# A shorter TensorE program in the experts' stage: one form of transposes, 512-wide gate and up products, one copy of the last down

## The chip, the core and the metric

The kernel runs on one core of one Trainium2 chip. The metric is the device time of one execution in microseconds; the time before is the median of three runs. The five engines each run a program of their own and meet at semaphores: TensorE (PE; its weight loads are shown apart as PEld), VectorE (DVE), ScalarE (ACT), GpSimd (POOL) and SyncE (SP). Line numbers are those of the kernel before.

## The reference

One layer of an encoder on 1024 tokens of width 1024 in float32: a mixer (neighbourhood attention, a bidirectional RWKV-7 scan, pooling), two layer norms, and a mixture of experts. Only the last is touched. Each token goes to two of 32 experts; the tokens of an expert are padded to blocks.

```python
order = jnp.argsort(e_flat)                      # assignments sorted by expert
padded = ((counts + MOE_BLOCK - 1) // MOE_BLOCK) * MOE_BLOCK
...
def expert_block(args):
    ti, e, wt = args
    xb = x_pad[ti]                               # the block's token rows, width 1024
    hb = jax.nn.silu(xb @ w_gate[e]) * (xb @ w_up[e])      # 1024 -> 512
    return (hb @ w_down[e]) * wt[:, None]                  # 512 -> 1024
y = lax.map(expert_block, (...))
out = jax.ops.segment_sum(y.reshape(total, d), buf_tok, num_segments=t + 1)[:t]
```

## The kernel before

The mixer and the router fill the first 949 us of the profiled span and are left as they are. Then `experts()` (line 1461) runs up to NP = 50 blocks. How many are used, and how many token rows each holds, is known only at run time: the router writes a code for each block (0 unused, 1 for 32 rows, 2 for 64, 3 for 128), and `size(e, g)` (line 1498) reads it into a register on every engine. The program is written out block after block, for each engine by itself; nothing loops. Wherever the work depends on the block's size, `by_size` (line 1511) writes it three times, for 128, 64 and 32 rows in this order, each behind a compare-and-branch that skips it when the code differs. The first SURE = 16 blocks are always used; from block 15 on, `go_on` (line 1516) tests whether the next block is used: its false side holds `end()`, which on PE is one more copy of the last block's down products in all three sizes, and its true side the next step, nested inside.

`pipeline` (line 1528) sets PE's order in step g:

1. `size(g+1)` (line 1499);
2. `head(g)`: gate and up products. For 128 rows (line 1689) two halves of 256 columns, each gate then up, 8 matmuls each into one PSUM bank; for 64 and 32 rows (line 1697) the token columns share the array, 16 and 32 matmuls;
3. `rows(g+1)` (line 1672): eight transposes of the gathered token rows, as many rows wide as the block;
4. `down(g-1)` (line 1717 for 128 rows, line 1728 for the others): 8, 8 or 16 matmuls;
5. `turn(g)` (line 1705): transposes of h = silu(gate)*up, four, four or two, in a shape of its own for 128 rows and for the smaller sizes.

A float32 matmul is two matmul records with a weight load each in the trace; a transpose is one of each. On ACT, `head` is the silu (lines 1765, 1768) and `turn` the copy of h's transpose out of PSUM (line 1773); on DVE, `head` is the product (lines 1789, 1793), and `out` scales the block's result into y (lines 1751, 1756). Both copy half of the token transposes (line 1738). Their semaphores count two updates for each block on `sil` and `h`.

SP loads the weights of block g into buffer set g % 3, gate, up (line 1559) and then the down matrix of block g-1, each 2 MB, with at most two under way (line 1558); a load whose expert is already there is skipped at run time. POOL gathers the token rows of block g+4 (line 1630) after it has sent the results of block g out (line 1638).

Of the kernel before, what the change touches and what calls it, by code (L numbers as in the profile page):

```python
# [12 lines left out]
AF = mybir.ActivationFunctionType  # L13
# [5 lines left out]
D = 1024  # L19
# [104 lines left out]
class Builder:  # L124
# [1336 lines left out]
    def experts(self):  # L1461
# [25 lines left out]
        names = ["T0", "T1", "xT", "gu0", "gu1", "sil", "h", "ht", "hs", "y0", "y1", "e0", "e1", "late", "g2", "o"]  # L1487
# [23 lines left out]
        def by_size(e, c, f):  # L1511
            for v, t in SIZES:
                with e.If(c == v):
                    f(t)
# [13 lines left out]
        def pipeline(e, rows, head, down, turn):  # L1528

            def step(g, old, c):  # L1530
                new = size(e, g + 1) if g + 1 < NP else None
                by_size(e, c, lambda t: head(g, t))
                if new is not None:
                    by_size(e, new, lambda t: rows(g + 1, t))
                if g and down:
                    by_size(e, old, lambda t: down(g - 1, t))
                if turn:
                    by_size(e, c, lambda t: turn(g, t))
                go_on(e, g, new, lambda: down and by_size(e, c, lambda t: down(g, t)), lambda k: step(k, c, new))

            c = size(e, 0)
            by_size(e, c, lambda t: rows(0, t))
# [7 lines left out]
        with nc.Block() as blk:  # L1550
# [113 lines left out]
            def _(e):  # L1664
                mm = e.matmul

                def rows(g, t):
                    e.wait_ge(sem(f"xg{g % NX}"), 16 * (g // NX + 1))
                    for hf in range(2):
                        for j in range(4):  # L1670
                            k = 4 * hf + j
                            i = e.transpose(pT[hf][:, t * j:t * j + t], xg[0:t, g % NX, k:D:8], ident[0:t, 0:t])  # L1672
                        i.then_inc(sem(f"T{hf}"), 1)
# [6 lines left out]
                def head(g, t):  # L1680
# [285 lines left out]
```

## Time and profile before

| what | value |
| --- | --- |
| median of three runs | 1594.07 us (1593.53 to 1601.02) |
| the profiled execution | 1595.89 us |
| its span | 1594.0 us |
| the experts' stage in the span | about 949 to 1537 us |
| matmul records / weight loads of PE in that stage | 3496 / 3496 |
| mean granted PE clock over the span | 0.915 |

The span is the time between the first and the last recorded instruction; the execution's own time is 1.9 us longer. A busy PE row says that matmuls were under way, and what idled ahead of a group is given with what ended it; "issue" there means that the trace shows no semaphore for which the engine waited. Compare-and-branch instructions are not counted as busy, but the view of one source line gives their durations. The DMA view lists the queue that brings the engines their instructions (kind "instruction").

### The profile page before, as it was taken

How to read it: one execution, taken by the hardware profiler on the slowest of the kernel's cores; microseconds unless marked ns; L12 is line 12 of the kernel's file. 1: busy time of each engine (PE TensorE's matmuls, PEld its weight loads, DVE VectorE, ACT ScalarE, POOL GpSimd, SP SyncE). 2: the span in 40 equal slices, each digit the busy share in tenths (PEclk: the TensorE clock that was granted, in tenths of full speed). 3: DMA queues.
4: the chain of work that ended last, by engine and by line, in shares of the span. 5: the costliest groups of instructions: out<-in, count | busy, mean ns of one | idle time of the engine just before them, and what ended most of it. 6: DMA issues, size and time to landing. Idle time of an engine off the chain costs nothing. (4 is left out here: it accounts for less than half of the span.)

```text
span 1594.0 us, 25797 instructions
## 1 busy us (share of the span) xinstructions
PE 1383.6 (87%) x8638; PEld 1014.9 (64%) x8638; DVE 779.3 (49%) x2015; ACT 573.9 (36%) x1196; POOL 379.0 (24%) x442
## 2 busy tenths in 40 slices
PE   6999999978869899899999728999998898789866
PEld 5778777766656677676788725676764575566522
DVE  6776786845974666655668851111111111111127
ACT  5663332414566777676444320000000010000006
POOL 3331332350347115601323141100110011101000
PEclk8999999987869899989999758999999999899978
DMA  9868999866413217117383648878978877887674
GB/s 256 221 195 309 290 296 332 285 221 179 134 51 105 80 41 204 39 53 219 95 322 121 250 173 353 338 296 305 376 275 310 334 298 279 333 337 307 253 268 201
DMA packets 163401, 371.94 MB, mean 233 GB/s; under 512 B 22880, under 2 KB 99009, under 8 KB 154227
## 3 DMA queue, kind: packets, MB, share of 16 engines
q1 hardware_dynamic: 155555, 350.59, 62.0%
q0 software_dynamic: 7632, 18.51, 3.6%
q8 instruction: 133, 2.18, 0.6%
q14 instruction: 81, 0.66, 0.1%
HBM read 365.47 MB, written 65.44 MB: 270 GB/s over the span
## 5 line engine op out<-in xcount | busy, mean ns | idle before, releaser
L1689 PE MATMUL m_pgu<-w,m_xT 128*128 128x256 f32 x896 | 200.1, 385 | 7.0 <-issue 7.0
L1689 PEld LDWEIGHTS m_pgu<-w,m_xT 128*128 128x128 f32 x896 | 171.5, 193 | 31.9 <-issue 8.2
L1697 PE MATMUL m_pgu<-w,m_xT 128*32 128x256 f32 (+1 forms) x1312 | 119.1, 459 | 38.8 <-issue 38.8
L1638 POOL DMA_INDIRECT ys_s<-m_y,m_idx x37 | 35.0, 946 | 494.4 <-DVE m_y L1756 299.9
L196 PE MATMUL pg<-uh,w_h 128*128 128x512 f32 x320 | 127.1, 404 | 2.2 <-ACT uh L294 1.6
L197 PE MATMUL pg<-ul,w_h 128*128 128x512 f32 x320 | 128.8, 402 | 0.2 <-POOL ul L295 0.2
L198 PE MATMUL pg<-uh,w_l 128*128 128x512 f32 x320 | 127.4, 398 | 0.0
L1697 PEld LDWEIGHTS m_pgu<-w,m_xT 128*32 128x32 f32 (+1 forms) x1312 | 56.6, 127 | 91.4 <-issue 76.4
L1789 DVE TENSOR_TENSOR m_h<-m_sil,m_pgu 128x256 f32<-128x256 f32 x28 | 11.8, 421 | 192.6 <-ACT m_sil L1765 192.6
L1717 PE MATMUL m_py<-w,m_hT 128*128 128x512 f32 x224 | 99.6, 597 | 0.0
L1793 DVE TENSOR_TENSOR m_h<-m_sil,m_pgu 64x256 f32<-64x256 f32 (+1 forms) x23 | 10.8, 471 | 160.2 <-ACT m_sil L1768 156.4
L1765 ACT ACTIVATE m_sil<-m_pgu 128x256 f32<-128x256 f32 x28 | 10.7, 383 | 196.1 <-PE m_pgu L1689 196.1
L210 DVE SCALAR_TENSOR_TENSOR acc<-wm,sc_c,acc 128x256 f32<-128x256 f32 x112 | 62.0, 554 | 31.9 <-DMA wm<-in_w_mod_dram 22.1
L1773 ACT COPY m_hT<-m_ph 128x128 f32<-128x128 f32 (+2 forms) x37 | 14.8, 401 | 165.3 <-PE m_ph L1705 165.3
L1717 PEld LDWEIGHTS m_py<-w,m_hT 128*128 128x128 f32 x224 | 41.4, 190 | 47.3 <-issue 46.9
L196 PEld LDWEIGHTS pg<-uh,w_h 128*128 128x128 f32 x320 | 61.0, 192 | 15.8 <-ACT uh L294 1.8
L197 PEld LDWEIGHTS pg<-ul,w_h 128*128 128x128 f32 x320 | 61.5, 192 | 14.4 <-POOL ul L295 0.9
L198 PEld LDWEIGHTS pg<-uh,w_l 128*128 128x128 f32 x320 | 61.4, 192 | 13.6 <-issue 0.7
L945 DVE SCALAR_TENSOR_TENSOR sn<-s,fc,sf 64x64 f32<-64x64 f32 x168 | 47.6, 283 | 41.8 <-PE s L936 38.7
L756 PE MATMUL g<-zi,bk 64*128 64x128 f32 x384 | 54.2, 319 | 15.2 <-DMA bk<-bkd 9.5
L1768 ACT ACTIVATE m_sil<-m_pgu 64x256 f32<-64x256 f32 (+1 forms) x23 | 9.8, 427 | 153.9 <-PE m_pgu L1697 153.9
L756 PEld LDWEIGHTS g<-zi,bk 64*128 64x128 f32 x384 | 46.5, 217 | 27.8 <-issue 10.3
(521 smaller groups left out, 3090.6 us busy)
## 6 DMA issues: line engine op xcount, KB each, us to landing
w<-in_moe_w_gate_dram SPq DMA_DIRECT2D x37, 2048.0 KB, 8.7
w<-in_moe_w_up_dram SPq DMA_DIRECT2D x37, 2048.0 KB, 12.9
w<-in_moe_w_down_dram SPq DMA_DIRECT2D x37, 2048.0 KB, 15.5
wm<-in_w_mod_dram SPq DMA_DIRECT2D x128, 128.0 KB, 4.5
w<-in_w_in_dram SPq DMA_DIRECT2D x21, 512.0 KB, 6.6
hd<-h SPq DMA_DIRECT2D x18, 512.0 KB, 4.5
wm<-in_w_mod_dram SPq DMA_DIRECT2D x16, 512.0 KB, 6.6
w<-ys_s SPq DMA_DIRECT2D x8, 1024.0 KB, 13.0
```

Of the source, the lines that this page charges most:

```text
L196: mm(out, lh[0], rh[0], start=start, stop=False)
L197: mm(out, lh[0], rh[1], start=False, stop=False)
L198: mm(out, lh[1], rh[0], start=False, stop=stop)
L210: nc.vector.scalar_tensor_tensor(acc, wm, self.sc_c[:, k:k + 1], acc, op0=OP.mult, op1=OP.add)
L756: nc.tensor.matmul(pa[h][:, j], bk[hs, j], zr[hs, j], start=True, stop=True)
L945: nc.vector.scalar_tensor_tensor(sn[H[h], H[h]], p[H[h], 2, H[h]], fc[H[h]], sf[H[h], H[h]], op0=OP.mult, op1=OP.add)
L1638: e.indirect_dma_start(out=self.ys_d, out_offset=off(idx[0:t, NP + g:NP + g + 1]), in_=y[0:t, g % NY], in_offset=None, bounds_check=2 * S ...
L1689: i = mm(pgu[q][:, o:o + 256], xT[:, k], w[:, k, 256 * q:256 * q + 256], start=k == 0, stop=k == 7)
L1697: i = mm(pgu[0][o:o + t, 0:n], xT[:, k, 0:t], w[:, k, c:c + n], start=k == 0, stop=k == 7)
L1717: i = mm(py[nh], hT[:, 128 * f:128 * f + 128], wd[b][:, f, 512 * nh:512 * nh + 512], start=f == 0, stop=f == 3)
L1773: e.copy(hT[:, 0:n], ph[:, 0:n]).then_inc(sem("hs"), 1)
L1789: e.tensor_mul(h[:, c], sil[:, c], pgu[q][:, 256:512]).then_inc(sem("h"), 1)
```

## The change

On PE the token transposes (`rows`) and the transposes of h (`turn`) are written once for all sizes, always 128 by 128; unused columns are not read afterwards. `turn` does two more transposes where the code is over 1. The gate and up products of 128 rows become 8 matmuls of 512 columns for the whole gate and 8 for the whole up; the up weights are waited for between the two. `by_size` writes the 32-row version first and puts the other two behind one more branch. The copy of the last down in `end()` goes: a step after the last used block runs its down, and the new `if_used` branches past what an unused block would do. The other engines follow: one silu and one product for 128 rows, one update per block on `sil` and `h`, copies that read the new strides, and h is set to zero once at the start of the stage. Loads, gathers and the down products keep their form.

```diff
         def by_size(e, c, f):
-            for v, t in SIZES:
-                with e.If(c == v):
-                    f(t)
+            with e.If(c == 1):
+                f(32)
+            with e.If(c > 1):
+                for v, t in SIZES[:2]:
+                    with e.If(c == v):
+                        f(t)
+
+        def if_used(e, c, g, f):
+
+            if g < SURE:
+                f()
+            else:
+                with e.If(c > 0):
+                    f()
...
             def step(g, old, c):
                 new = size(e, g + 1) if g + 1 < NP else None
-                by_size(e, c, lambda t: head(g, t))
+                head(g, c)
                 if new is not None:
-                    by_size(e, new, lambda t: rows(g + 1, t))
+                    rows(g + 1, new)
                 if g and down:
                     by_size(e, old, lambda t: down(g - 1, t))
                 if turn:
-                    by_size(e, c, lambda t: turn(g, t))
-                go_on(e, g, new, lambda: down and by_size(e, c, lambda t: down(g, t)), lambda k: step(k, c, new))
+                    turn(g, c)
+                if g + 1 == NP:
+                    if down:
+                        by_size(e, c, lambda t: down(g, t))
+                elif down:
+                    if_used(e, c, g, lambda: step(g + 1, c, new))
+                else:
+                    if_used(e, new, g + 1, lambda: step(g + 1, c, new))
 
             c = size(e, 0)
-            by_size(e, c, lambda t: rows(0, t))
+            rows(0, c)
             step(0, None, c)
...
-                def rows(g, t):
-                    e.wait_ge(sem(f"xg{g % NX}"), 16 * (g // NX + 1))
-                    for hf in range(2):
-                        for j in range(4):
-                            k = 4 * hf + j
-                            i = e.transpose(pT[hf][:, t * j:t * j + t], xg[0:t, g % NX, k:D:8], ident[0:t, 0:t])
-                        i.then_inc(sem(f"T{hf}"), 1)
+                def rows(g, c):
+
+                    def turn_all():
+                        e.wait_ge(sem(f"xg{g % NX}"), 16 * (g // NX + 1))
+                        for hf in range(2):
+                            for j in range(4):
+                                k = 4 * hf + j
+                                i = e.transpose(pT[hf][:, 128 * j:128 * j + 128], xg[:, g % NX, k:D:8], ident)
+                            i.then_inc(sem(f"T{hf}"), 1)
+                    if_used(e, c, g, turn_all)
...
-                def head(g, t):
+                def head(g, c):
+                    by_size(e, c, lambda t: gate_up(g, t))
+
+                def gate_up(g, t):
                     b, n = g % NB, g // NB + 1
                     e.wait_ge(sem("xT"), 2 * g + 2)
                     e.wait_ge(sem(f"G{b}"), 16 * n)
-                    e.wait_ge(sem(f"U{b}"), 16 * n)
                     if t == 128:
-                        for q in range(2):
-                            for w, o in ((wg[b], 0), (wu[b], 256)):
-                                for k in range(8):
-                                    i = mm(pgu[q][:, o:o + 256], xT[:, k], w[:, k, 256 * q:256 * q + 256],
-                                           start=k == 0, stop=k == 7)
+                        for q, w in enumerate((wg[b], wu[b])):
+                            if q:
+                                e.wait_ge(sem(f"U{b}"), 16 * n)
+                            for k in range(8):
+                                i = mm(pgu[q], xT[:, k], w[:, k], start=k == 0, stop=k == 7)
                             i.then_inc(sem(f"gu{q}"), 1)
                     else:
+                        e.wait_ge(sem(f"U{b}"), 16 * n)
                         n = 8 * t
                         e.sem_inc(sem("gu0"), 1)
...
-                def turn(g, t):
-
-                    e.wait_ge(sem("h"), 2 * g + 2)
-                    n, r = (512, 128) if t == 128 else (8 * t, 64)
-                    for j in range(n // 128):
-                        i = e.transpose(ph[:, r * j:r * j + r], h[0:r, 128 * j:128 * j + 128], ident[0:r, 0:r])
-                    i.then_inc(sem("ht"), 1)
+                def turn(g, c):
+
+                    def part(js):
+                        for j in js:
+                            i = e.transpose(ph[:, 128 * j:128 * j + 128], h[:, 128 * j:128 * j + 128], ident)
+                        return i
+
+                    def both():
+                        e.wait_ge(sem("h"), g + 1)
+                        with e.If(c > 1):
+                            part((2, 3))
+                        part((0, 1)).then_inc(sem("ht"), 1)
+                    if_used(e, c, g, both)
...
-                    pT[hf][:, 0:4 * t].rearrange("p (k t) -> p k t", k=4)).then_inc(sem("xT"), 1)
+                    pT[hf].rearrange("p (k t) -> p k t", k=4)[:, :, 0:t]).then_inc(sem("xT"), 1)
...
                 def head(g, t):
+                    e.wait_ge(sem("gu0" if t == 128 else "gu1"), g + 1)
                     if t == 128:
-                        for q in range(2):
-                            e.wait_ge(sem(f"gu{q}"), g + 1)
-                            e.activation(sil[:, 256 * q:256 * q + 256], pgu[q][:, 0:256], AF.Silu).then_inc(sem("sil"), 1)
+                        i = e.activation(sil, pgu[0], AF.Silu)
                     else:
-                        e.wait_ge(sem("gu1"), g + 1)
-                        e.activation(sil[0:64, 0:8 * t], pgu[0][64:128, 0:8 * t], AF.Silu).then_inc(sem("sil"), 2)
+                        i = e.activation(sil[0:64, 0:8 * t], pgu[0][64:128, 0:8 * t], AF.Silu)
+                    i.then_inc(sem("sil"), 1)
 
                 def turn(g, t):
-                    n = 512 if t == 128 else 4 * t
                     e.wait_ge(sem("ht"), g + 1)
-                    e.copy(hT[:, 0:n], ph[:, 0:n]).then_inc(sem("hs"), 1)
+                    if t == 128:
+                        i = e.copy(hT, ph)
+                    else:
+                        n = t // 16
+                        i = e.copy(hT[:, 0:64 * n].rearrange("p (j t) -> p j t", j=n),
+                                   ph.rearrange("p (j t) -> p j t", j=4)[:, 0:n, 0:64])
+                    i.then_inc(sem("hs"), 1)
...
+                    e.wait_ge(sem("sil"), g + 1)
                     if t == 128:
-                        for q in range(2):
-                            e.wait_ge(sem("sil"), 2 * g + 1 + q)
-                            c = slice(256 * q, 256 * q + 256)
-                            e.tensor_mul(h[:, c], sil[:, c], pgu[q][:, 256:512]).then_inc(sem("h"), 1)
+                        e.wait_ge(sem("gu1"), g + 1)
+                        i = e.tensor_mul(h, sil, pgu[1])
                     else:
                         n = 8 * t
-                        e.wait_ge(sem("sil"), 2 * g + 2)
-                        e.tensor_mul(h[0:64, 0:n], sil[0:64, 0:n], pgu[0][0:64, 0:n]).then_inc(sem("h"), 2)
-
-                pipeline(e, lambda g, t: evac_T(e, g, t, 1), head, lambda g, t: [out(e, g, t, q) for q in range(2)], None)
+                        i = e.tensor_mul(h[0:64, 0:n], sil[0:64, 0:n], pgu[0][0:64, 0:n])
+                    i.then_inc(sem("h"), 1)
+
+                def sized(f):
+                    return lambda g, c: by_size(e, c, lambda t: f(g, t))
+
+
+                e.memset(h, 0.0).then_inc(sem("h0"), 1)
+                e.wait_ge(sem("h0"), 1)
+                pipeline(e, sized(lambda g, t: evac_T(e, g, t, 1)), sized(head),
```

## Rows read from the trace of the kernel before

**Rows 1.** The page's chain that ended last, by engine.

```profile
PE 33%; issue 4%; DMA 2%; DVE 1%; ACT 0%; POOLq 0%; POOL 0%; DVEq 0%; SPq 0%; ACTq 0%
```

**Rows 2.** Stretches: length, busy PE PEld DVE ACT POOL, clock, DMA share, GB/s.

```profile
0.00:949.00 949.00, 825.78 (x5070) 659.45 (x5070) 651.92 (x1745) 494.18 (x1020) 308.03 (x368) 0.90 0.58 187
949.00:1537.00 588.00, 524.39 (x3496) 340.95 (x3496) 95.45 (x198) 54.12 (x135) 70.05 (x73) 0.95 0.80 309
```

**Rows 3.** PE's groups by shape, 949 to 1537: busy, mean ns | idle before.

```profile
L1689 PE MATMUL m_pgu<-w,m_xT 128*128 128x256 f32 x896 | 200.1, 385 | 7.0 <-issue 7.0
...
L1697 PE MATMUL m_pgu<-w,m_xT 128*32 128x256 f32 x1152 | 80.0, 434 | 29.0 <-issue 29.0
L1697 PE MATMUL m_pgu<-w,m_xT 128*64 128x512 f32 x160 | 39.1, 638 | 9.8 <-issue 9.8
```

**Rows 4.** PE in order of time, undisturbed: start us, us, line, count.

```profile
1083.31 14.08 PE L1689 MATMUL m_pgu<-w,m_xT 128*128 128x256 f32 x64
...
1098.35 1.93 PE L1728 MATMUL m_py<-w,m_hT 128*32 128x256 f32 x32
1100.21 0.66 PE L1705 MATMUL m_ph<-cst,m_h 128*128 128x128 f32 x4
1101.18 7.09 PE L1697 MATMUL m_pgu<-w,m_xT 128*64 128x512 f32 x32 [0.31 <-issue]
1108.20 1.07 PE L1672 MATMUL m_pT<-cst,m_xg 32*128 32x32 f32 x8
1109.19 7.13 PE L1717 MATMUL m_py<-w,m_hT 128*128 128x512 f32 x16
...
1116.65 3.66 PE L1697 MATMUL m_pgu<-w,m_xT 128*32 128x256 f32 x64
1120.24 1.16 PE L1672 MATMUL m_pT<-cst,m_xg 128*128 128x128 f32 x8
1122.12 3.65 PE L1728 MATMUL m_py<-w,m_hT 128*64 128x512 f32 x16 [0.73 <-issue]
```

**Rows 5.** PE's waits, 949 to 1537: us in total, times, longest us.

```profile
PE m_pgu L1697 <- issue: 38.8, 17, 7.2
PE m_pT L1672 <- DMA m_xg<-u_s,m_idx: 8.1, 2, 7.0
PE m_pgu L1689 <- issue: 7.0, 8, 2.6
...
PE m_ph L1705 <- issue: 3.0, 2, 1.9
```

**Rows 6.** Line 1513's branches, 949 to 1537: count, ns min/median/max.

```profile
L1513 PEldq COMPARE_BRANCH  x447: 68/207/4559, 950.6 to 1530.4; - x149
...
L1513 DVEq COMPARE_BRANCH  x336: 43/56/76, 950.5 to 1535.8; - x168
```

**Rows 7.** Instruction queue, packets, MB: 0 to 949, 949 to 1186, 1186 to 1537.

```profile
q8 instruction: 40, 0.66, 0.3%
...
q8 instruction: 33, 0.54, 0.9%
...
q8 instruction: 58, 0.95, 1.1%
```

**Rows 8.** PE in order of time, with stalls (idle before in brackets).

```profile
1358.95 6.14 PE L1697 MATMUL m_pgu<-w,m_xT 128*32 128x256 f32 x64 [7.17 <-issue]
...
1370.89 15.72 PE L1689 MATMUL m_pgu<-w,m_xT 128*128 128x256 f32 x64 [2.58 <-issue]
```

**Rows 9.** Instruction queue again: 1333 to 1371 and 1403 to 1417.

```profile
q8 instruction: 7, 0.11, 1.2%
...
q8 instruction: 3, 0.05, 1.4%
```

**Rows 10.** SyncE's queue waits, 949 to 1537: us, times, longest us.

```profile
SPq L1558 <- DMA w<-in_moe_w_gate_dram: 165.8, 25, 9.5
```

**Rows 11.** Gathers of line 1630, 949 to 1537: issue to landing.

```profile
DMA to landing us min/median/max: 3.7/7.1/8.7
```

More of the change, by code (lines that the diff above doesn't have):

```diff
@@ L1486, in experts @@
         sems = {}
-        names = ["T0", "T1", "xT", "gu0", "gu1", "sil", "h", "ht", "hs", "y0", "y1", "e0", "e1", "late", "g2", "o"]
+        names = ["T0", "T1", "xT", "gu0", "gu1", "sil", "h", "h0", "ht", "hs", "y0", "y1", "e0", "e1", "late", "g2", "o"]
         names += [f"l{i}" for i in range(8)] + ["x1a", "x1b", "tail_pe", "tail_act", "tail_dve"]
@@ L1761, in head @@
                 def head(g, t):
+                    e.wait_ge(sem("gu0" if t == 128 else "gu1"), g + 1)
                     if t == 128:
-                        for q in range(2):
-                            e.wait_ge(sem(f"gu{q}"), g + 1)
-                            e.activation(sil[:, 256 * q:256 * q + 256], pgu[q][:, 0:256], AF.Silu).then_inc(sem("sil"), 1)
-                    else:
-                        e.wait_ge(sem("gu1"), g + 1)
-                        e.activation(sil[0:64, 0:8 * t], pgu[0][64:128, 0:8 * t], AF.Silu).then_inc(sem("sil"), 2)
+                        i = e.activation(sil, pgu[0], AF.Silu)
+                    else:
+                        i = e.activation(sil[0:64, 0:8 * t], pgu[0][64:128, 0:8 * t], AF.Silu)
+                    i.then_inc(sem("sil"), 1)
                 def turn(g, t):
-                    n = 512 if t == 128 else 4 * t
                     e.wait_ge(sem("ht"), g + 1)
-                    e.copy(hT[:, 0:n], ph[:, 0:n]).then_inc(sem("hs"), 1)
+                    if t == 128:
[7 more added lines that the diff above has]
+                    return lambda g, c: by_size(e, c, lambda t: f(g, t))
                 e.activation(sil[0:1, 0:1], ident[0:1, 0:1], AF.Silu)
-                pipeline(e, lambda g, t: evac_T(e, g, t, 0), head, None, turn)
+                pipeline(e, sized(lambda g, t: evac_T(e, g, t, 0)), sized(head), None, sized(turn))
                 tail(e, "act")
@@ L1784, in head, with sized @@
                     wait(e, "ht", g)
+                    e.wait_ge(sem("sil"), g + 1)
                     if t == 128:
-                        for q in range(2):
-                            e.wait_ge(sem("sil"), 2 * g + 1 + q)
-                            c = slice(256 * q, 256 * q + 256)
-                            e.tensor_mul(h[:, c], sil[:, c], pgu[q][:, 256:512]).then_inc(sem("h"), 1)
+                        e.wait_ge(sem("gu1"), g + 1)
+                        i = e.tensor_mul(h, sil, pgu[1])
                     else:
                         n = 8 * t
-                        e.wait_ge(sem("sil"), 2 * g + 2)
-                        e.tensor_mul(h[0:64, 0:n], sil[0:64, 0:n], pgu[0][0:64, 0:n]).then_inc(sem("h"), 2)
-                pipeline(e, lambda g, t: evac_T(e, g, t, 1), head, lambda g, t: [out(e, g, t, q) for q in range(2)], None)
+                        i = e.tensor_mul(h[0:64, 0:n], sil[0:64, 0:n], pgu[0][0:64, 0:n])
+                    i.then_inc(sem("h"), 1)
+                def sized(f):
+                    return lambda g, c: by_size(e, c, lambda t: f(g, t))
+                e.memset(h, 0.0).then_inc(sem("h0"), 1)
+                e.wait_ge(sem("h0"), 1)
+                pipeline(e, sized(lambda g, t: evac_T(e, g, t, 1)), sized(head),
+                         lambda g, t: [out(e, g, t, q) for q in range(2)], None)
                 tail(e, "dve")
```

## The prediction

> **What bounds the kernel now.** First the page's chain of work that ended last: PE holds 33% of the span, and 4%, some 64 us, is "issue", time for which no semaphore accounts [rows 1]. Next the busy time by stretch. In the 588.00 us of the experts' stage PE is busy for 524.39 us at a mean clock of 0.95 of full speed, DVE for 95.45 and ACT for 54.12 [rows 2]. So PE sets the pace, and it idles for 588.00 - 524.39 = 63.6 us.
>
> Then the groups by shape, whose counts give the blocks: 896 / 64 = 14 of 128 rows, 1152 / 64 = 18 of 32 and 160 / 32 = 5 of 64 [rows 3]; below, large, small and mid. The undisturbed stretch gives their own pace, start to start: products 14.0, 7.05 and 3.6 us for large, mid and small, down 7.05, 3.6 and 1.9, eight token transposes 1.0, four transposes of h 0.6, two of them 0.3 [rows 4]. That is 22.65, 12.25 and 6.8 us for a step, and 14 x 22.65 + 5 x 12.25 + 18 x 6.8 = 501 us for all. PE is busy 23 us longer than that. A stretch with stalls [rows 8] shows why: ahead of a small block it idles 7.17 us, and the same 64 matmuls then take 6.14 us where they take 3.66 undisturbed; a large one takes 15.72 for 14.08. [...]
>
> The waits of PE tell where the idle time lies: 38.8 us in 17 waits ahead of mid and small products, 7.0 in 8 ahead of large ones, 3.0 ahead of the transposes of h, 8.1 for gathers, nearly all of it (7.0) the very first [rows 5]. The groups split the 38.8 into 29.0 small and 9.8 mid [rows 3]. No semaphore explains them, but the branches do: those of line 1513 take at most 76 ns on DVE, and on PE up to 4559 [rows 6]. On PE the target's instructions are not there yet. The instruction queue brought 40 packets before 949 us [rows 7], while PE ran 5070 matmuls and 5070 loads [rows 2]: about 250 instructions a packet, 16.4 KB; call it a page. In the stage it brought 33 + 58 = 91 pages [rows 7]. Where PE stalls in row, 7 pages take 38 us, 5.4 us each; in a short stretch 3 took 14 us, 4.7 each [rows 9].
>
> So each page costs PE about 5 us unless work lasts that long. The program before has, for a step, 128 + 64 + 128 instructions of products, 48 + 128 of transposes and down, 20 for h, and some 26 waits and branches: 542, or 2.15 pages; from block 15 on 134 more for the copy of the last down, 2.7 pages. 15 x 2.15 + 22 x 2.7 = 92, against 91 brought. A small step works 6.8 us, and 2.7 pages ask for 14.6.
>
> **The change part by part.** *Length.* The products shrink to 64 + 64 + 128, the token transposes to 16, those of h to 8, and the copy of the last down goes: 408 and 26, 1.7 pages. 37 steps ask for 63 pages, 28 fewer.
>
> *Small blocks.* Their stalls are 29.0 us ahead of the products and most of 3.0 and of 6.7 spread elsewhere (63.6 - 8.1 - 38.8 - 7.0 - 3.0); I count 34. A small step now needs 2.5 pages in the mean (7 at 2.15, 11 at 2.7): at 5.4 us it overruns its own work by 6.7, afterwards by 9.2 - 6.8 = 2.4. I let the stalls shrink in that proportion: 34 becomes 12, **22 us less**. Ends: 34 (no stall left) and 10 (in proportion to the pages alone).
>
> *Mid blocks.* 9.8 us. Pages fall to 9.2 us, below the step's 12.25, but ahead of their products lie now two skipped versions (130 + 65 instructions) instead of one. I take half, **5 less**, between 0 and 9.8.
>
> *Large blocks.* Here the change speaks against itself. Their version came first and was reached without a jump; now the 32-row version, 130 instructions or half a page, is skipped just ahead of 14 large products. Before, the 23 mid and small blocks skipped about 0.7 page each at that place, and 17 stalled, for 2.3 us each: 2.4 us for each page skipped. Half a page in 14 blocks gives 17 us; with shorter steps a page has longer to come, so I scale it by 1.7 / 2.5 to **11 more**. Ends: none, and 14 x 2.3 = 32.
>
> *Clock.* The 23 us of slow matmuls came with 55 us of stalls. With 22 + 5 - 11 = 16 us of stalls gone, 23 x 16 / 55 = **7 less**; ends 0 and 23.
>
> *Wide products.* Sixteen records of 512 columns take 7.13 us in the down products, so 32 take 14.2, where 64 of 256 columns take 14.08 [rows 4]: **1.5 more** over 14 blocks, bounds -1.5 and +3. The up weights are waited for half a product later, which can only help.
>
> *Transposes.* Eight of 32 by 32 take 1.07 us and eight of 128 by 128 1.16 [rows 4]: 0 to 2 us more over 23 blocks, and I take **1**. Those of h keep their count, at 0.6 us for four: nothing, within 1 us.
>
> *The wait in `turn`.* It stands ahead of a branch now, so it holds PE's sequencer, and behind it queue the transposes of h, the next size and branches and the next products. ACT and DVE take 54.12 / 135 and 95.45 / 198, 0.4 and 0.5 us for an instruction [rows 2], so h is ready 0.9 us after the last product, while PE still has 1.0 us of token transposes and 1.9 to 7.05 of down ahead of it: nothing. Without that cover it would be 0.9 us a step, 33 in all.
>
> *The end.* The last down lies one head version set (some 260 instructions, a page) behind the last turn: **3 more**, between 0 and a branch and a page, 4.6 + 5.4. DVE's one memset hides under the first gather wait of 7.0 us.
>
> The sum: -22 - 5 + 11 - 7 + 1.5 + 1 + 3 = -17.5, and for the branches that go (three tests for the rows become none or one; the median on PE is 207 ns [rows 6]) another 2: **-20 us**. Against the profiled execution, 1595.89 - 20 = 1576; on the median of 1594.07, 1574.
>
> [...]
>
> **The rivals.** (1) The forecast: stalls shrink but stay. (2) The pages stop binding: 63 pages at 5.4 are 340 us, far below PE's 501, so all but the first stalls could vanish, 50 us of idle time and most of the 23: 1594 - 50 to 73, about 1521 to 1548. For it: large steps of 22.65 us leave time for four pages. Against it: a page is asked for late, else the packets of 2.7 pages would be hidden in the large steps too, and 7.0 us there say they are not. (3) Slower: large blocks stall ahead of their products as mid and small ones did, and the clock drops with them [rows 8]: 2.3 us of stall and up to 1.6 of slow matmuls, 2.8 to 3.9 for each of 14. The sum holds 11 us, 0.8 for each; it comes to nothing at 11 + 20 = 31 us, so the rival decides from 2.2 us a large block. At 2.8 to 3.9 it is 8 to 24 us slower, 1602 to 1618. For it: the jump is now where small blocks paid. Against it: a large step before it, or a down of 7.05 us, gives a page its 5 us. (4) No change: something else is next. Gathers land after 3.7 to 8.7 us [rows 11], and a gather is issued some two steps before its use, 13.6 us where both are small; SP waited 165.8 us for gate loads under way [rows 10], at a DMA share of 0.80 [rows 2]. If weights or gathers come late by what PE gains, 1586 to 1600. Against it: only 1.1 of the 8.1 us of gather waits fell later than the first, and no wait for weights shows.
>
> **How the numbers follow.** (1) 0.58, (2) 0.15, (3) 0.10, (4) 0.17. The forecast's own range is 1558 to 1586: the lower end has no stall of small blocks left (12 us more) and 4 us of clock with it, the upper one their lower saving of 10. Eight in ten reach from 1545, into rival 2, to 1592, into rival 4. This kernel's measurement tells about 0.5%, 8 us: faster is below 1586, all of (2) and all but 0.02 of (1), and a little of (4): 0.73; same 0.17; slower 0.10.
>
> **What would show it.** The instruction queue brings some 63 pages in the stage, not 91; if it is over 80, the length was misjudged. PE's branches still reach over 2 us, but idle time ahead of small and mid products falls from 38.8 to about 17, and ahead of large ones rises from 7.0 to about 18. If large ones stay at 7 and small ones near zero, rival 2 holds; if gathers (line 1672) or ACT name the waits, rival 4. Large products keep 14.1 us for 32 records.

## The result and the profile after

| | before | after |
|---|---|---|
| median of 4 runs, us | 1597.41 (1593.53 to 1601.02) | 1570.03 (1565.44 to 1580.58) |
| profiled execution, us | 1595.89 | 1565.44 |
| its span, us | 1594.0 | 1563.6 |
| experts' stage, us | 581.3 | 553.4 |
| PE busy in it, us | 524.4 | 509.7 |
| PE idle in it, us | 56.9 | 43.7 |
| pages of instructions in it | 91 | 66 |

The ratio is 0.9858, with a 95% interval from 0.9821 to 0.9895: 27 us less. The stage is counted here from its first token transposes to the end of its last down (954.4 to 1535.7 us before, 951.9 to 1505.3 after). Of the 30.4 us of span it holds 27.9; 2.5 are gained ahead of it, and the 58.3 us behind it are the same in both.

The chain that ended last, by engine, is still PE's; its share of "issue" fell from 4% to 3% [rows 1]:

```profile
PE 34%; issue 3%; DVE 1%; DMA 1%; ACT 0%; POOLq 0%; DVEq 0%; SPq 0%
```

The stretch of the stage (length; busy PE, PEld, DVE, ACT, POOL with counts; clock, DMA share, GB/s) against the second row of [rows 2]. PE has 448 matmuls fewer, the mean clock is 0.97 for 0.95, and the DMA share is 0.84 for 0.80:

```profile
949.00:1510.00 561.00, 509.74 (x3048) 252.78 (x3048) 94.88 (x192) 50.44 (x120) 70.99 (x74) 0.97 0.84 323
```

The instruction queue in the same stretch, against 33 + 58 packets [rows 7]:

```profile
q8 instruction: 66, 1.08, 0.8%
```

PE's waits in the stage (us in total, times, longest), against [rows 5]:

```profile
PE m_py L1758 <- issue: 12.2, 4, 7.3
...
PE m_py L1747 <- issue: 9.6, 4, 3.0
PE m_pgu L1721 <- issue: 8.3, 6, 4.6
PE m_pgu L1713 <- issue: 7.2, 4, 2.7
PE m_pT L1692 <- DMA m_xg<-u_s,m_idx: 6.4, 1, 6.4
PE m_ph L1728 <- issue: 4.7, 4, 2.0
```

Ahead of mid and small products (line 1721) stand 8.3 us where there were 38.8, ahead of large ones (line 1713) 7.2 where there were 7.0. What is new stands ahead of the down products (lines 1747 and 1758): 21.8 us, against 3.6 before, and 4.7 ahead of the transposes of h, against 3.0. The row of before for the down products:

```profile
PE m_py L1728 <- issue: 3.6, 4, 1.8
```

All issue idle together (the rows above, and 0.8 ahead of token transposes) is 42.8 us, against 55.

PE's groups by shape (busy, mean ns | idle before), against [rows 3]:

```profile
L1713 PE MATMUL m_pgu<-w,m_xT 128*128 128x512 f32 x448 | 197.0, 598 | 7.4 <-issue 7.2
L1747 PE MATMUL m_py<-w,m_hT 128*128 128x512 f32 x224 | 98.7, 594 | 9.6 <-issue 9.6
L1721 PE MATMUL m_pgu<-w,m_xT 128*32 128x256 f32 x1152 | 68.9, 389 | 1.9 <-issue 1.4 <-DVE m_xT L1768 0.5
...
L1721 PE MATMUL m_pgu<-w,m_xT 128*64 128x512 f32 x160 | 39.1, 642 | 6.9 <-issue 6.9
L1758 PE MATMUL m_py<-w,m_hT 128*32 128x256 f32 x576 | 35.4, 382 | 0.8 <-issue 0.8
L1758 PE MATMUL m_py<-w,m_hT 128*64 128x512 f32 x80 | 21.2, 677 | 11.4 <-issue 11.4
```

The small products lost nearly all of their stalls (29.0 to 1.4), and with them their slow matmuls: 80.0 us of busy time became 68.9, where 18 undisturbed sets of 3.66 us need 65.9. How slow they were shows in the trace of before: in the first 3 us behind the stall of 7.17 us [rows 8], 1359 to 1362 us, the granted clock was 0.50 and a small matmul took 634 ns at the median; in an undisturbed set, 1116.65 to 1120.3 us, the clock was 1.00 and a matmul took 379 ns.

One place where the time now goes, in PE's order (start, length, line, count, idle before in brackets), the counterpart of [rows 4]:

```profile
1043.69 13.96 PE L1713 MATMUL m_pgu<-w,m_xT 128*128 128x512 f32 x32
1057.48 1.05 PE L1692 MATMUL m_pT<-cst,m_xg 128*128 128x128 f32 x8
1058.37 7.03 PE L1747 MATMUL m_py<-w,m_hT 128*128 128x512 f32 x16
1065.24 0.60 PE L1728 MATMUL m_ph<-cst,m_h 128*128 128x128 f32 x4
1065.77 3.66 PE L1721 MATMUL m_pgu<-w,m_xT 128*32 128x256 f32 x64
1069.36 1.16 PE L1692 MATMUL m_pT<-cst,m_xg 128*128 128x128 f32 x8
1072.49 7.10 PE L1747 MATMUL m_py<-w,m_hT 128*128 128x512 f32 x16 [1.97 <-issue]
```

The branches on PE next to that gap, of line 1514 (the test for more than 32 rows) from 1068.2 to 1068.5 us and of line 1512 (the test for 32) from 1068.5 to 1068.7 (count, ns, start):

```profile
L1514 PEldq COMPARE_BRANCH  x1: 220/220/220, 1068.3 to 1068.3; - x1
...
L1512 PEldq COMPARE_BRANCH  x1: 3338/3338/3338, 1068.6 to 1068.6; - x1
```

Behind a small block's products the sequencer jumps over the 128-row and 64-row versions, at 1068.3 us; it meets eight transposes, and at 1068.6 it jumps again, over the 32-row version of down, since the block whose down is next is a large one. The second jump takes 3.34 us. PE has work until 1069.36 + 1.16 = 1070.52 and then stands until 1072.49. The same pattern, small products and then a down of 64 or 128 rows, holds all the other stalls of these two groups but the very last: 1.79, 2.83 and 3.02 us ahead of large ones, 2.21 and 1.88 ahead of mid ones. The pattern comes ten times in the stage, and four times it has no stall.

That the jump waits for its page can be seen in the trace. While it lasts, one packet of the instruction queue starts, between 1069.5 and 1069.6 us:

```profile
q8 instruction: 1, 0.02, 61.2%
```

Its share, 61.2% of 16 engines' time in a window of 0.1 us, is 0.98 us. So the packet has been moved at about 1070.5, and the branch ends at about 1071.9, 1.4 us later. This holds throughout the stage: in the trace of the kernel before, all 27 branches of PE that take over 1 us end 1.2 to 1.8 us after such a packet, and in the changed kernel all 16 end 1.3 to 1.6 us after one.

### The profile page after: what moved, and what is told of

It reads as the page before. It is cut to its first block, busy times and chain, and to the rows that moved or that the text cites. A ratio compares the mean times of both kernels' runs of the same rounds, so it can differ in the third digit from the quotient of the medians.

```text
span 1563.6 us, 24661 instructions
## 1 busy us (share of the span) xinstructions
PE 1367.4 (87%) x8190; PEld 923.9 (59%) x8190; DVE 778.7 (50%) x2002; ACT 571.8 (37%) x1182; POOL 380.4 (24%) x442
## 5 line engine op out<-in xcount | busy, mean ns | idle before, releaser
L1713 PE MATMUL m_pgu<-w,m_xT 128*128 128x512 f32 x448 | 197.0, 598 | 7.4 <-issue 7.2
L1713 PEld LDWEIGHTS m_pgu<-w,m_xT 128*128 128x128 f32 x448 | 84.7, 192 | 110.4 <-issue 110.3
L1721 PE MATMUL m_pgu<-w,m_xT 128*32 128x256 f32 (+1 forms) x1312 | 108.0, 420 | 8.7 <-issue 8.3
L1825 DVE TENSOR_TENSOR m_h<-m_sil,m_pgu 128x512 f32<-128x512 f32 x14 | 9.6, 688 | 192.4 <-PE m_pgu L1713 192.4
L1747 PEld LDWEIGHTS m_py<-w,m_hT 128*128 128x128 f32 x224 | 41.5, 190 | 57.1 <-issue 57.1
L1758 PE MATMUL m_py<-w,m_hT 128*32 128x256 f32 (+1 forms) x656 | 56.6, 418 | 12.2 <-issue 12.2
L1781 DVE TENSOR_TENSOR m_y<-m_py,m_g 128x512 f32<-128x512 f32 x28 | 19.4, 692 | 88.0 <-PE m_py L1747 88.0
L1786 DVE TENSOR_TENSOR m_y<-m_py,m_g 32x256 f32<-32x256 f32 (+1 forms) x82 | 37.0, 451 | 52.3 <-PE m_py L1758 51.1
```

What stands on the lines that cost most here:

```text
L1713: i = mm(pgu[q], xT[:, k], w[:, k], start=k == 0, stop=k == 7)
L1721: i = mm(pgu[0][o:o + t, 0:n], xT[:, k, 0:t], w[:, k, c:c + n], start=k == 0, stop=k == 7)
L1747: i = mm(py[nh], hT[:, 128 * f:128 * f + 128], wd[b][:, f, 512 * nh:512 * nh + 512], start=f == 0, stop=f == 3)
L1758: i = mm(py[0][o:o + t, 0:n], hT[:, 64 * j + t * a:64 * j + t * a + t], wd[b][:, f, c:c + n], start=f == 0, stop=f == 3)
L1786: i = e.tensor_mul(y[0:t, g % NY, c], py[0][t * j:t * j + t, 0:n], g2[0:t, c])
```

## The experiments

All twelve were timed in three rounds beside the kernel before, four kernels to a job; its medians in the three jobs were 1593.19, 1593.6 and 1589.52 us. The issue idle is summed from PE's waits in the stage. Differences below are of the medians; by the ratios, each against the kernel before beside it, they come out up to 6 us smaller or larger (x_flat against the changed kernel: 41 us by the medians, 36 by the ratios).

| kernel | median, us | ratio, 95% | PE busy | PE idle | issue idle | pages |
|---|---|---|---|---|---|---|
| before | 1597.41 | | 524.4 | 56.9 | 55 | 91 |
| after | 1570.03 | 0.9858 (0.9821, 0.9895) | 509.7 | 43.7 | 42.8 | 66 |
| b_wide | 1567.43 | 0.9847 (0.979, 0.9903) | 515.0 | 37.9 | 33.2 | 82 |
| b_wide_pad | 1589.82 | 1.0015 (0.9978, 1.0051) | 518.2 | 53.4 | 50.3 | 92 |
| b_form | 1570.6 | 0.9859 (0.98, 0.9918) | 514.1 | 41.5 | 37.6 | 84 |
| b_nocopy | 1567.17 | 0.9839 (0.9809, 0.987) | 512.7 | 39.4 | 38.4 | 82 |
| b_order | 1663.1 | 1.0452 (1.0394, 1.051) | 548.7 | 98.1 | 94.0 | 92 |
| x_flat | 1528.8 | 0.9632 (0.9584, 0.9681) | 499.4 | 10.5 | 4.1 | 63 |
| x_headflat | 1535.8 | 0.9655 (0.96, 0.9709) | 502.2 | 16.5 | 15.0 | 65 |
| x_narrow | 1554.16 | 0.9775 (0.9708, 0.9843) | 510.3 | 29.6 | 28.1 | 75 |
| x_shift | 1556.26 | 0.9786 (0.9756, 0.9816) | 508.2 | 28.4 | 25.6 | 63 |
| x_flat_shift | 1528.94 | 0.9617 (0.955, 0.9685) | 498.8 | 11.8 | 8.5 | 64 |
| x_pad | 1637.32 | 1.0292 (1.0264, 1.0321) | 525.1 | 88.2 | 86.3 | 86 |
| x_flat_pad | 1580.14 | 0.9932 (0.9899, 0.9965) | 518.8 | 47.1 | 46.1 | 86 |

Names that begin with b are the kernel before with one thing changed, those with x the changed kernel. Theory A throughout is the forecast's: PE waits for pages of its program.

### The order of the sizes

The diff also turns the order of the versions around: before, 128, 64, 32 stood side by side; now 32 stands first and the other two lie in a block behind it. x_flat gives the changed kernel the old order, on all engines:

```diff
-            with e.If(c == 1):
-                f(32)
-            with e.If(c > 1):
-                for v, t in SIZES[:2]:
-                    with e.If(c == v):
-                        f(t)
+            for v, t in SIZES:
+                with e.If(c == v):
+                    f(t)
```

> The changed kernel with the three sizes in the order of before again: 128 rows first, then 64, then 32, one test each. Theory A (PE waits for pages of its program; what counts is the program's length and where parts are skipped): the length stays about 1.7 pages a step, but large products are reached without a jump, as before, and small ones lie behind 131 skipped instructions. The 7.2 us ahead of large products should go to about 2, the stalls ahead of the down products (21.8 us) change place; the sum of the stalls, 43 us, may end between 15 and 55 us, the time between 1540 and 1585 us. Theory B (the gain came from cheaper work, wider matmuls and fewer records, and the place of the sizes is nothing): 1570 us within 4.

It took 1528.8 us, 41 less than the changed kernel, below the lowest time that A had allowed. The waits of its PE:

```profile
PE m_pT L1689 <- DMA m_xg<-u_s,m_idx: 8.8, 2, 6.9
PE m_pgu L1718 <- issue: 2.4, 2, 1.3
PE m_py L1755 <- DVE m_y L1783: 2.1, 1, 2.1
PE m_pgu L1718 <- DMA w<-in_moe_w_up_dram: 1.7, 1, 1.7
...
PE m_py L1755 <- issue: 1.7, 2, 1.4
```

Issue idle is down to 4.1 us, and for the first time PE waits for weights, if only 1.7 us. The same blocks as above, in the trace of x_flat:

```profile
1057.73 3.66 PE L1718 MATMUL m_pgu<-w,m_xT 128*32 128x256 f32 x64
1061.32 1.17 PE L1689 MATMUL m_pT<-cst,m_xg 128*128 128x128 f32 x8
1062.33 7.03 PE L1744 MATMUL m_py<-w,m_hT 128*128 128x512 f32 x16
```

The gap of 1.97 us ahead of the large down isn't there. In this order nothing is left to skip behind a small block's products, nor ahead of a large down, and the branches on PE nearby (line 1513) take at most 415 ns:

```profile
L1513 PEldq COMPARE_BRANCH  x9: 68/209/415, 1050.1 to 1063.7; - x9
```

b_order does the reverse: the kernel before gets the new order (the diff above read backwards), and nothing else.

> The kernel before with the order of sizes alone taken from the change: the 32-row version first, the other two behind one more branch. No work and no length changes (two branches more in a step). Theory A, as it stands after the first four runs (a skipped part costs PE what its queue of waiting matmuls doesn't cover; behind a large block's products that is several us, ahead of them or behind a small block's products about one): large blocks are now reached over a skip and small ones skip with little cover, so the stalls rise well above the 55 us of before, and the time is 1630 to 1680 us. Theory C (the order costs only the 11 us that the prediction put on the large blocks, since small blocks gain what large ones lose): 1585 to 1607 us.

1663.1 us, 69.5 more than the kernel before beside it, as A said. Its pages are 92, one more than before, so it isn't by more pages that the order costs. PE's waits and its stage (columns as above):

```profile
PE m_pgu L1692 <- issue: 30.9, 11, 7.6
PE m_pgu L1700 <- issue: 22.4, 11, 5.7
PE m_py L1720 <- issue: 17.2, 5, 4.8
PE m_pT L1675 <- issue: 12.0, 4, 5.2
```

```profile
949.00:1599.00 650.00, 547.62 (x3492) 351.21 (x3494) 94.20 (x196) 54.20 (x135) 70.13 (x73) 0.90 0.73 279
```

Ahead of large products (line 1692) stand 30.9 us, where the kernel before has 7.0: 11 stalls of 2.8 us. The third rival had named 2.3 us of stall for each of 14 large blocks, 32 us in all. With them the mean clock falls to 0.90, and the busy time rises by 24 us.

x_headflat narrows it down: the old order for PE's gate and up products alone, all else as in the changed kernel.

```diff
-                    by_size(e, c, lambda t: gate_up(g, t))
+                    in_order(e, c, lambda t: gate_up(g, t))
```

> The changed kernel with the order 128, 64, 32 for PE's gate and up products alone; the down products, and all other engines, keep the 32-row version first. Theory A: most of the 41 us between the changed kernel and the run with the old order everywhere comes from the skip ahead of the products and behind a small block's products, so 1528 to 1545 us; the stalls ahead of the large products (7.2 us) and of the down products (21.8 us) both go below 6. If the order of the down versions is what counts, 1555 to 1572 us.

1535.8 us, 34 of the 41. PE's waits for its own program:

```profile
PE m_py L1764 <- issue: 7.5, 1, 7.5
...
PE m_pgu L1727 <- issue: 6.2, 6, 2.6
...
PE m_pgu L1719 <- issue: 0.2, 1, 0.2
```

The 7.5 us are the last down of the stage, the longest wait of line 1758 in the changed kernel too; in x_flat the last down waits 2.1 us, for DVE. All other stalls ahead of down products are gone, although down keeps its order and a large one is still reached by a jump over the 32-row version. The instruction queue brought 65 pages, one fewer than in the changed kernel, but only 2 branches of PE take over 1 us, both at the very end of the stage; in the changed kernel it is 16. This points to the two jumps in short order: without the one behind the small products, the other found its target there. It doesn't prove it, for the edit also moves the code, and x_shift, below, loses the same stalls with both jumps kept.

### Each shortening by itself

Three kernels give the kernel before, in its own order, one of the three shortenings. b_wide has the 512-wide gate and up products, with one silu, one product and one update of each semaphore:

```diff
-                        for q in range(2):
-                            for w, o in ((wg[b], 0), (wu[b], 256)):
...
+                        for q, w in enumerate((wg[b], wu[b])):
...
+                            for k in range(8):
+                                i = mm(pgu[q], xT[:, k], w[:, k], start=k == 0, stop=k == 7)
```

> The kernel before with the 512-wide gate and up products of 128-row blocks alone. Their own pace stays (14.08 us for 64 records of 256 columns, 14.0 for 32 of 512 in the changed kernel); the step loses 64 instructions, a quarter of a page. Theory A: about 82 pages in place of 91, the stalls fall by a third to a half, 1555 to 1580 us. Theory B (the width itself is worth something or nothing, the length nothing): 1590 to 1597 us.

b_form has the one form of transposes, with the narrow products and the copy of the last down kept:

```diff
-                    n, r = (512, 128) if t == 128 else (8 * t, 64)
-                    for j in range(n // 128):
-                        i = e.transpose(ph[:, r * j:r * j + r], h[0:r, 128 * j:128 * j + 128], ident[0:r, 0:r])
...
+                        with e.If(c > 1):
+                            part((2, 3))
+                        part((0, 1)).then_inc(sem("ht"), 1)
```

> The kernel before with the one form of token transposes and of h's transposes alone; order of sizes, 256-wide products and the copy of the last down as before. Some 50 instructions fewer in a step, a fifth of a page; the small blocks' transposes grow to 128 by 128, at most 2 us in all. The wait for h moves onto a branch. Theory A: about 83 pages, 1560 to 1585 us. Theory B: 1592 to 1597 us.

b_nocopy has one copy of the last down:

```diff
-                go_on(e, g, new, lambda: down and by_size(e, c, lambda t: down(g, t)), lambda k: step(k, c, new))
+                if g + 1 == NP:
+                    if down:
+                        by_size(e, c, lambda t: down(g, t))
+                elif down:
+                    if_used(e, c, g, lambda: step(g + 1, c, new))
...
```

> The kernel before, with the copy of the last down products taken away alone: one more step after the last used block runs them, as in the changed kernel. No work changes; from block 15 on a step is 542 instructions in place of 676, 2.1 pages in place of 2.7. Theory A: about 80 pages in place of 91, the stalls fall from 55 us to 30 to 40 and the slow matmuls with them, 1560 to 1582 us. Theory B: no work was saved, 1594 us within 5.

They gave 26.2, 23.0 and 26.0 us, as A said, with 9, 7 and 9 pages fewer. Each one alone brings about as much as the whole change. None of the three was run with its code moved, which was worth 14 us in the changed kernel (x_shift), and only the wide products were set against a pad of their length. All three in the old order are x_flat: 64 us for 28 pages. The three sum to 75, so little of what one saves is taken from another, and the end of it is near: PE's busy time in x_flat, 499 us, is the 501 us that the prediction had found as the stage's own time.

### Length or width

b_wide_pad tells the two sides of the wide products apart. It is b_wide with its program made as long again as before, by 62 transposes in a block that is never run, and its branch, behind the products of each step:

```diff
+                def skipped(e, n, c):
+                    with e.If(c > 3):
+                        for _ in range(n // 2):
+                            e.transpose(ph[:, 0:128], ident, ident)
...
+                skipped(e, 62, c)
```

> The kernel before with the 512-wide products of 128-row blocks alone, and 62 instructions with their branch behind the products in each step, always skipped, so that a step is as long as before. Theory A (the 26 us of the wide products are their 64 instructions fewer): back to 1583 to 1610 us, about 90 pages in the stage. Theory B (they are the width's): 1564 to 1572 us.

1.0015 (0.9978 to 1.0051): nothing is left of b_wide's 26 us. Its queue and its stage:

```profile
q8 instruction: 92, 1.51, 1.0%
```

```profile
949.00:1531.00 582.00, 521.17 (x3063) 258.42 (x3062) 93.82 (x190) 51.74 (x121) 70.07 (x73) 0.96 0.81 312
```

In the stage PE runs 448 matmuls fewer than in the kernel before and is busy for 518.2 us against 524.4, 1.2% less; in the time of the whole none of it is left. To within the interval, half a per cent, the wide form gains by its length alone.

x_narrow asks the same from the other end: x_flat with the 256-wide products back (the diff of b_wide read backwards).

> The changed kernel with the order 128, 64, 32 everywhere and 256-wide products of 128-row blocks again: 64 instructions more in a step (about 498, 1.95 pages), with the large blocks' own pace as before. Where hardly a stall is left (the run with the old order, 1529 us), theory A lets the longer step cost a few us only: 1530 to 1548 us. If the width has a worth of its own of the size seen from the kernel before (26 us), 1550 to 1560 us.

1554.16 us, 25 over x_flat, and above what A had allowed. The time lies in the range of the rival by which the width is worth something of its own, but b_wide_pad speaks against that rival, and the trace has 28.1 us of issue idle where x_flat has 4.1. 64 instructions a step, 12 pages (63 to 75), cost 2.1 us each, no more than pages cost elsewhere below, so A's price for them was too low. Another reading is that queued wide matmuls cover a jump for longer. In the changed kernel the sequencer was through with a large set of products at 1049.8 us, and PE worked on it until 1043.69 + 13.96 = 1057.65, 7.9 us longer; in the kernel before, with narrow ones, it was through at 1059.0, and PE at 1049.02 + 14.05 = 1063.07, 4.1 us later. The rows that follow, PE's branches of line 1516 from 1047 to 1058 us (after) and of line 1513 from 1056 to 1062 (before), have this in their first start. That the longer lead is worth time wasn't shown:

```profile
L1516 PEldq COMPARE_BRANCH  x2: 71/144/216, 1049.8 to 1053.7; - x2
```

```profile
L1513 PEldq COMPARE_BRANCH  x6: 68/208/353, 1059.0 to 1060.8; - x6
```

### Length and place alone

Four kernels add nothing but instructions that are never executed. x_pad puts 142 of them into each step of the changed kernel, behind `turn`:

```diff
                     turn(g, c)
+                skipped(e, 142, c)
```

> The changed kernel with 142 instructions and their branch added to every step of PE behind the transposes of h, always skipped: no work is added, the step is 577 instructions long, 2.3 pages in place of 1.7. Theory A: the queue brings about 90 pages in the stage in place of 66, the stalls rise from 43 us to 70 or more, and the time is 1592 to 1620 us, so length alone takes back all the gain. Theory B: one branch more in a step, hidden: 1570 to 1575 us.

1637.32 us, 67 over the changed kernel and beyond what A had allowed. Its waits:

```profile
PE m_pgu L1715 <- issue: 35.9, 11, 5.0
PE m_pgu L1723 <- issue: 21.9, 10, 5.6
PE m_ph L1730 <- issue: 11.3, 5, 3.3
PE m_py L1760 <- issue: 10.7, 4, 6.5
```

Now the stalls are ahead of large products (line 1715), 35.9 us in 11, 3.3 each, as in b_order. With the short program of the changed kernel the same jump is cheap, 7.2 us in 4; with a long one it costs about what the third rival said, 32 us in all.

x_flat_pad does the same to x_flat.

> The changed kernel with the order 128, 64, 32 everywhere, and 142 instructions with their branch behind the transposes of h in each step, always skipped: 575 instructions, 2.25 pages. In the changed kernel itself the same length cost 67 us. Theory A: less here, since only this skip lies without cover: 1550 to 1590 us, about 85 pages. If length costs the same whatever the order, 1590 to 1600 us.

1580.14 us, 51 over x_flat, as A said. So 142 instructions a step cost 51 us in the old order and 67 in the new one, for 23 and 20 pages: 2.2 and 3.4 us a page.

x_shift puts 150 skipped instructions into the changed kernel once, ahead of the stage, so that all that follows on PE stands 154 places further on in the code; x_flat_shift does it to x_flat with 98 (102 places).

```diff
+                skipped(e, 150, size(e, 0))
                 pipeline(e, rows, head, down, turn)
```

> The changed kernel with 150 instructions on PE that are skipped once, ahead of the stage, where PE waits 6.4 us for the first gather anyway; all later instructions stand 154 places (0.6 page) further on. Theory A: the boundaries of the pages fall elsewhere in each step, so the stalls come at other places: those ahead of the down products (21.8 us) and of the products (15.5 us) change by more than 10 us in all, in either direction, and the time lies outside 1565 to 1575 us, about 1545 to 1590. Theory B: nothing changes, 1570 us within 4, and the same waits at the same blocks.

> The changed kernel with the order 128, 64, 32 everywhere, and 98 instructions skipped once ahead of the stage on PE (102 places, 0.4 page). Theory A: with the skips under cover, where the pages' boundaries fall matters little: 1529 us within 6, where the same kind of shift moved the changed kernel by 14. Against it: 1535 to 1550 us, if 1529 was luck of the boundaries.

The changed kernel so moved took 1556.26 us, 14 us less with more in its program; the ratios, 0.9786 against 0.9858, make it 11. x_flat stayed at 1528.94. Both are as A said. PE's waits ahead of down products in x_shift:

```profile
PE m_py L1758 <- issue: 6.0, 1, 6.0
...
PE m_py L1747 <- issue: 0.5, 1, 0.5
```

The 6.0 us are the last down. So of the ten places with two jumps in short order none of the six that stalled in the changed kernel does so here, and one of the others stalls, for 0.5 us; the jumps are all still there. A pair of jumps is thus not enough: where the code stands decides whether it costs (21.8 us ahead of down products as it stood, 6.5 as moved), and why it costs in one place and not in the other wasn't shown. It also means that the price of the order in the changed kernel isn't one number: 41 us as the two stood, 27 after the two moves (1556.26 against 1528.94). Where many jumps leave PE without instructions (42.8 us of issue idle in the changed kernel), place was worth half of what the change itself brought, 14 of 27 us; in x_flat, where hardly any do (4.1 us), nothing.

## Why the prediction was right, and where its terms were not

The forecast was 1574 us and -20 us; measured were 1570.03 and, in the two profiled executions, -30.4 (1595.89 to 1565.44). The mechanism, by which PE waits for pages of its own program and less program means less waiting, holds: a program lengthened by code that never runs pays 22 to 67 us (b_wide_pad, x_flat_pad, x_pad), and long branches end just behind the packets that bring pages. That the total is so near is luck in part. The clock gave back twice what was forecast, the order cost more than forecast and elsewhere, and the same kernel moved by 154 places takes 1556 us, just outside the forecast's own range of 1558 to 1586.

**Pages.** 63 forecast for the stage, 66 brought. The 28 fewer a step-count gave are exact in the old order (x_flat, 63).

**Small and mid blocks.** -27 us of stalls forecast; ahead of their products 38.8 became 8.3, 30.5 less, where about 17 us were expected to remain. The small ones lost nearly all (29.0 to 1.4), more than the 22 forecast, the mid ones 2.9 (9.8 to 6.9), fewer than the 5: the sum was near, its parts less so.

**Large blocks.** 11 us more were forecast ahead of their products, within 0 to 32. There was nothing more (7.0 to 7.2). This is the step that failed, in its place and in its size. The prediction looked for the cost of the new order ahead of the products that are now reached by a jump. In the changed kernel it stands at the next jump behind small products, and so ahead of down (3.6 to 21.8 us, 7.3 of it the last) and of the transposes of h (3.0 to 4.7): the prediction had counted the versions skipped ahead of a product set, one by one, and not how close two jumps follow each other. x_headflat points to the pair, and x_shift shows that the pair costs only in some places. And the order costs 41 us in the changed kernel (27 in x_shift's place), 69.5 in the kernel before, not 11. At the length of the kernel before, or of x_pad, the stalls of 2.8 and 3.3 us did come where the prediction sought them.

**What length saves.** 27 us of stalls and 7 of clock were taken as the whole of it, less 11 for the order. The runs show 64 in the old order (x_flat), less 41 for the new one. The estimate in proportion to the overrun (2.4 us of 6.7 left) took pages at 5.4 us each. That is the spacing of packets in a stretch with dense stalls, PE's work included [rows 9], not what one costs: the packet of the 3.34 us branch took 0.98 us to move, and in the runs a page more costs 2.1 to 3.4 us of time in the mean, with some pages hidden under work. At 5.4 us a small step of 1.7 pages would still overrun its work; x_flat, with 63 pages and 4.1 us of issue idle in all, shows that it doesn't.

**Clock.** -7 forecast, with the ends 0 and 23; the busy time fell by 14.7. The rule, slow matmuls in proportion to stalls, gave 23 x 13 / 55 = 5 for the 13 us of idle time that went. The term came out at half of what was measured: the slow matmuls stood mostly behind the stalls of small blocks (80.0 to 68.9 us of products), which went almost wholly, and the new gaps of some 2 us before a large down cost little pace (7.10 us where 7.03 is undisturbed). The granted clock of before was 0.50 in the first 3 us behind the stalls of 7.17 and 2.58 us [rows 8]; in the changed kernel it was 1.00 in the 7.1 us behind the stall of 1.97.

**Wide products, transposes, the wait in `turn`.** 14.2 us for 32 wide records forecast, 13.96 measured, for 14.08 in the narrow form; the width by itself is worth nothing (b_wide_pad). Eight token transposes take 1.05 to 1.16 us, four of h 0.60 to 0.66, as forecast. Two of h, for small blocks, take 0.38 to 0.44 us where they took 0.33, and all of h 19.8 us where they took 17.7: 2 us more, where nothing within 1 was forecast. The wait in `turn` does hold PE's sequencer: in 10 of 37 blocks the branch behind it (line 1733) starts 0.04 us after DVE has finished h. But no wait on ACT or DVE for h appears among PE's waits.

**The end.** +3 forecast, up to 10. The last down waits 7.33 us in the changed kernel: within the bounds, but at the upper half. It came with the missing copy, not with the order: b_nocopy (8.2 us), x_narrow (8.0) and x_flat_shift (4.3) wait there in the old order, and of the kernels with the copy none waits there for instructions. In x_flat alone the copy is gone and the wait too, save 2.1 us for DVE.

**The rivals.** The second, in which the pages stop binding, was given 1521 to 1548 us (1544 by its own working, 1594 - 50) and 0.15. Its sign, large products at 7 us of idle time and small ones near zero, came true in the changed kernel (7.2 and 1.4), and yet the pages still bind there: the sign looked ahead of the products alone, and the stalls now stand ahead of down. In time the changed kernel isn't with this rival, but x_flat is, with 1528.8: the three shortenings do that much, and the order keeps 41 us of it back. The third, in which large blocks stall ahead of their products for 2.3 us each, is true of the order by itself (b_order), and was outweighed. The fourth began to show only in x_flat (and x_flat_shift), with 1.7 us for weights at a DMA share of 0.89:

```profile
949.00:1463.00 514.00, 499.42 (x3048) 247.67 (x3048) 93.18 (x184) 50.48 (x119) 70.10 (x73) 0.99 0.89 345
```

That less program brings no time, as this rival has it, the runs contradict: the changed kernel is 27 us faster and x_flat 64, and 142 instructions a step that are only jumped over cost 51 and 67 us. How much of the pages shows as idle time differs from kernel to kernel: x_flat brings 63 with 4.1 us of issue idle, the kernel before 91 with 55 us.

What stays open: x_narrow's 25 us were not parted into pages and cover, no run changed the work between two jumps alone, x_headflat wasn't moved, and which places in the code make a jump wait wasn't worked out.

The version that beats both kernels is x_flat: 1528.8 us, 0.9632 (0.9584 to 0.9681) of the kernel before.

## What to carry to other kernels

Where an engine idles for "issue" and its branches take microseconds (here 55 us of idle time, and branches of up to 4.56 us [rows 6]), count the pages of its program for a step against the work of that step, and shorten the code, also code that is never run. Among versions under conditions, look where two jumps follow each other with little work between: here the order in which the version with the most work stands first and the one with the least last leaves nothing to jump over behind the least work, and it was worth 27 to 41 us in the changed kernel, where each shortening gave 23 to 26. Where such stalls bind, move the program by some hundred instructions before a difference of 1% between two kernels is believed: here 154 places were worth 14 us of 1570.

## What the runs showed of the hardware

- Instructions that are never executed cost time: 142 a step, 20 to 23 pages in all, 51 to 67 us.
- The same pages cost differently by order: 91 and 92 of them in the stage of the kernel before and of b_order, with 55 and 94 us of issue idle, and a mean clock of 0.95 and 0.90.
- A jump that takes 0.2 us at the median took 3.34 us when another jump had come 0.3 us earlier. Six of ten such pairs stalled PE in the changed kernel, one in x_shift, with the same jumps in another place.
- Branches of PE that took over 1 us ended 1.2 to 1.8 us after a packet of 16.4 KB of the instruction queue had been moved: 27 of 27 in the kernel before, 16 of 16 in the changed one.
- A move of the stage's code on PE by 154 places, and 150 instructions skipped once, made the time 14 us shorter.
- A 512-wide f32 product takes what two 256-wide ones take: 13.96 us for 32 records, 14.08 for 64.
